# The second inverse of a block inversion taken by transposition, with 64-row and 64-column products and later modulation sums

## The chip, the cores and the metric

The kernel runs on 1 core of one Trainium2 chip. The metric is the device time of one execution in microseconds (us). Three runs of the kernel before gave 1495.1, 1495.2 and 1495.76 us, so the median is 1495.2 us.

## The reference, cut to what matters

The reference is two transformer blocks over 256 tokens of width 1024. The part that is changed belongs to the first block: an RWKV-7 recurrence of 8 heads of 64, and, beside it, the modulation vector that scales and shifts the layer norms.

```
mod = jax.nn.silu(c) @ cond_w + cond_b                   # 6 x 1024 sums over 1024
...
def step(state, inp):                                    # for each token and head
    r_t, w_t, k_t, v_t, kk_t, a_t = inp
    sa = jnp.einsum('bhvk,bhk->bhv', state, -kk_t)
    state = (state * w_t[:, :, None, :]
             + sa[..., None] * (kk_t * a_t)[:, :, None, :]
             + v_t[..., None] * k_t[:, :, None, :])
    y_t = jnp.einsum('bhvk,bhk->bhv', state, r_t)
    return state, y_t
```

Cut into two blocks of 128 tokens, the recurrence becomes matrix work. For each of 16 units (2 blocks of tokens by 8 heads) the sums `sa` solve a triangular system of 128 equations, and the kernel inverts its matrix.

## The kernel before

**The stage.** The block inversion fills roughly 105 to 216 us of the span. First `amat` (L588 to L594) makes score products for two units at a time: `AB`, from which the matrix is cut, and `AK`. A product has 128 rows, of which the 64 of the other head are zero in `AR`, and 256 columns. The DVE masks the result. The inverse is then built by doubling the size of the inverted blocks: level `li` from 0 to 6, four groups `g` of four units each. `TT` holds the inverse (transposed) and `TN` the other orientation, and both are carried along.

**One step** is one level of one group. `lvW` (L620) multiplies the level's off-diagonal part `off` by `TN` on the PE (L624), and the ACT copies the product to `W` (L625). The POOL cuts the next level's `off` (L609). `lvD` (L630) multiplies `TT` by `W` (L633) and the DVE adds it to `TN` (L634); it multiplies `W` by `TT` (L637) and the DVE adds that to `TT` (L638). At the last level, 6, `TN` is no longer needed. So there are 20 full steps (levels 1 to 5) and 4 of the last level. They are called s0 to s19 here, and a step is dated by the start of its addition to `TN`.

**Beside it.** The loop of L700 to L712 runs `lvW` one step ahead of `lvD`. After each `lvD` it takes one piece of `side()` (L668): first the `AK` score products, then transposes to token order (L649, L683), then the products `akv` (L658) of `AK` with values `vN`. After every second one it calls `modblk` (L309): a DMA of 512 KB into one of the three buffers of `wraw`, and a DVE multiplication with a running sum (L307). At `k == 10` it also does the layer norm of the convolution branch (L289 to L301 and L713 to L720), with three table loads on the ACT.

**Order.** Each engine runs its instructions strictly in an order that is fixed when the program is built. It is not the order in which the code is written: a scheduler sets it, so most of the 24 sums of L307 stand earlier than the loop calls them. A float32 product of 128 columns is two matmul records in the trace, and a transpose is one.

Of the kernel before, what the change touches and what calls it, by code (L numbers as in the profile page):

```python
# [15 lines left out]
AF = mybir.ActivationFunctionType  # L16
OP = mybir.AluOpType
AX = mybir.AxisListType

P = 128  # L20
T = 256
# [130 lines left out]
def r3(ap, b):  # L152
    return ap.rearrange("p (b t) -> p b t", b=b)
# [3 lines left out]
def body(ctx: ExitStack, tc: tile.TileContext, A: dict, out: bass.AP):  # L157
    nc = tc.nc
    pe, act, dve, pool, sp = nc.tensor, nc.scalar, nc.vector, nc.gpsimd, nc.sync
# [5 lines left out]
    def bank(name="bk"):  # L165
        return pp.tile([P, 512], F32, tag="bk", name=name)
# [9 lines left out]
    def con(name):  # L176
        w, o, n = CONST_OFF[name]
        return cst[w][:, o : o + n]
# [6 lines left out]
    ident, ones, bones = con("ident"), con("ones"), con("bones")  # L185
# [83 lines left out]
    def hs(h):  # L269
        return slice((h % 2) * 64, (h % 2) * 64 + 64)  # L270
# [38 lines left out]
    def modblk(b, c_row, junk):  # L309
        modmul(wraw(A["cond"][:, b]), b, c_row, junk)  # L310
# [16 lines left out]
    with ExitStack() as c1:  # L327
        pa = c1.enter_context(tc.tile_pool(name="pa", bufs=1))

        def tl(shape, name, tag=None, dt=F32, bufs=1):  # L330
            return (ph0 if tag in ("X3", "X4") else pa).tile(shape, dt, tag=tag or name, name=name, bufs=bufs)
# [57 lines left out]
        ps = bank()  # L389
# [4 lines left out]
        ps = bank()  # L394
# [86 lines left out]
        bT, ktT = X4[:, 0], X4[:, 1]  # L481
# [10 lines left out]
        AR = tl([P, 2, 4, 2, 2, P], "AR")  # L492
# [25 lines left out]
        for tb in range(2):  # L518
            ps = bank()
# [3 lines left out]
        for hp in range(4):  # L523
            ps = bank()
# [50 lines left out]
        for hp in range(4):  # L575
            ps = bank()
# [8 lines left out]
        AB = tl([P, 16, 2, P], "ABt", "AB")  # L585
        mskb = con("msk")[:, None, :].to_broadcast([P, 2, 256])

        def amat(src, dst, u0):  # L588
            ps = bank()
            for uu in range(2):  # L590
                u = u0 + uu
                tb, h = u // 8, u % 8
                pe.matmul(ps[:, uu * T : (uu + 1) * T], src[:, h // 2, tb * P : (tb + 1) * P], AR[:, h % 2, h // 2, tb].rearrange("p a t -> p (a t)"), start=True, stop=True)
            dve.tensor_tensor(dst[:, u0 : u0 + 2].rearrange("p u a t -> p u (a t)"), r3(ps, 2), mskb, op=OP.mult)  # L594


        TT = tl([P, 16, P], "TT", "X1")
        TN = tl([P, 16, P], "TN", "X2")
        W = tl([P, 16, P], "W", "X3")
# [3 lines left out]
        def gsl(g):  # L603
            return slice(g * 4, g * 4 + 4)

        def lv_off(li, g):
            off = tl([P, 4, P], "off", bufs=4)
            lv = con("lvl")[:, li * P : li * P + P]
            pool.tensor_tensor(off, AB[:, gsl(g), 0, :], lv[:, None, :].to_broadcast([P, 4, P]), op=OP.mult)  # L609
            offs[li, g] = off  # L610

        def lv0(g):
            off = offs[0, g]
            dve.tensor_tensor(TT[:, gsl(g)], off, idb, op=OP.add)
            ps = bank()
            for uu in range(4):
                pe.matmul(ps[:, uu * P : (uu + 1) * P], off[:, uu], ident, start=True, stop=True)
            dve.tensor_tensor(TN[:, gsl(g)], r3(ps, 4), idb, op=OP.add)

        def lvW(li, g):  # L620
# [8 lines left out]
        def lvD(li, g):  # L629
            if li < 6:  # L630
                ps2 = bank()
                for uu in range(4):
                    pe.matmul(ps2[:, uu * P : (uu + 1) * P], TT[:, g * 4 + uu], W[:, g * 4 + uu], start=True, stop=True)  # L633
                dve.tensor_tensor(TN[:, gsl(g)], TN[:, gsl(g)], r3(ps2, 4), op=OP.add)  # L634
            ps1 = bank()
            for uu in range(4):
                pe.matmul(ps1[:, uu * P : (uu + 1) * P], W[:, g * 4 + uu], TT[:, g * 4 + uu], start=True, stop=True)  # L637
            dve.tensor_tensor(TT[:, gsl(g)], TT[:, gsl(g)], r3(ps1, 4), op=OP.add)  # L638


        vN = tl([P, 2, 512], "vN")
        bN = tl([P, 512], "bN")
        kN = tl([P, 512], "kN")
        RH0 = tl([P, 8, 64], "RH0")

        def to_tok(srcs, dst):
            ps = bank()
            for hp in range(4):
                pe.transpose(ps[:, hp * P : (hp + 1) * P], srcs(hp), ident)  # L649
            act.activation(dst, ps, AF.Copy)  # L650

        def akv(g):
            ps = bank()
            tb = g // 2
            for uu in range(4):
                u = g * 4 + uu
                hp = (u % 8) // 2
                pe.matmul(ps[:, uu * P : (uu + 1) * P], AK[:, u, 0], vN[:, tb, hp * P : (hp + 1) * P], start=True, stop=True)  # L658
            h0 = (g % 2) * 4
            for pr in range(2):  # L660
                src = ps.rearrange("p (h r n) -> p h r n", h=2, r=4)[:, :, 3 * pr]
                if tb == 0:
                    dst = RH0[:, h0 : h0 + 4].rearrange("p (h r) n -> p h r n", r=2)[:, :, pr]
                else:
                    dst = RH1[:, h0 : h0 + 4].rearrange("p (h r) x n -> p h r x n", r=2)[:, :, pr, 1]
                act.activation(dst, src, AF.Copy)

        def side():  # L668

            for u0 in range(0, 16, 2):  # L670
                amat(ktT, AK, u0)
                yield
            for tb in range(2):
                to_tok(lambda hp: vT[:, hp, tb * P : (tb + 1) * P], vN[:, tb])
                yield
            to_tok(lambda hp: bT[:, hp, 0:P], bN)
            yield
            to_tok(lambda hp: ktT[:, hp, 0:P], kN)
            yield
            for pr in range(2):  # L680
                ps = bank()
                for hp in range(4):
                    pe.transpose(ps[:, hp * P : (hp + 1) * P], AR[:, pr, hp, 1, 0], ident)  # L683
                act.activation(RH1.rearrange("p (h r) x n -> p r h x n", r=2)[:, pr, :, 0], ps.rearrange("p (h r n) -> p r h n", h=4, r=2)[:, pr], AF.Copy)
                yield
            for g in range(4):
                akv(g)
                yield

        for u0 in range(0, 16, 4):  # L690
            amat(bT, AB, u0)
            amat(bT, AB, u0 + 2)
            lv_off(0, u0 // 4)
        sd = side()
        for g in range(4):
# [4 lines left out]
        AK = tl([P, 16, 2, P], "AKt", "AK")  # L700
        RH1 = tl([P, 8, 2, 64], "RH1")
# [3 lines left out]
        for k, (li, g) in enumerate(todo):  # L705
            if k + 1 < len(todo):
                lvW(*todo[k + 1])
            lvD(li, g)
            next(sd, None)
            if k % 2:  # L710
                modblk(next(mrest), c_row, junk)
            if k == 10:  # L712

                xcc, sqc = tl([P, 4, T], "xcc", "vT"), tl([P, 4, T], "sqc", "ug")
                rstdc = layer_norm(pa, yc, xcc, sqc, 4, "conv")
                ychi, yclo = tl([P, 4, T], "ychi", "yc", F32R), tl([P, 4, T], "yclo", "ug", F32R)
                for b in range(4):
                    dve.tensor_tensor(xcc[:, b], xcc[:, b], rstdc, op=OP.mult)
                    act.activation(xcc[:, b], xcc[:, b], AF.Silu, scale=col("conv_ln_g", b), bias=col("conv_ln_b", b))
                    asplit(ychi[:, b], yclo[:, b], xcc[:, b])  # L720
# [9 lines left out]
        HG = tl([P, 16, 2, 64], "HG", "X4")  # L730
        for g in range(4):
            ps = bank()
            for uu in range(4):
                u = g * 4 + uu
                h = u % 8
                if g < 2:
                    rhs = RH0[:, h - h % 2 : h - h % 2 + 2].rearrange("p a n -> p (a n)")
                else:
                    rhs = RH1[:, h].rearrange("p a n -> p (a n)")
                pe.matmul(ps[:, uu * P : (uu + 1) * P], TT[:, u], rhs, start=True, stop=True)  # L740
            if g < 2:
                for pr in range(2):
                    src = ps.rearrange("p (h r n) -> p h r n", h=2, r=4)[:, :, 3 * pr]
                    act.activation(HG[:, g * 4 : g * 4 + 4].rearrange("p (h r) x n -> p h r x n", r=2)[:, :, pr, 1], src, AF.Copy)
            else:
                act.activation(HG[:, g * 4 : g * 4 + 4].rearrange("p u a n -> p u (a n)"), r3(ps, 4), AF.Copy)


        Sb = tl([P, 4, P], "Sb", "RH0")
# [2 lines left out]
        ps = bank()  # L752
        for hp in range(4):
            o = ps[:, hp * P : (hp + 1) * P]
# [8 lines left out]
        ps = bank()  # L763
# [8 lines left out]
        for tb in range(2):  # L772
            ps = bank()
            for h in range(8):
                u = tb * 8 + h
                o = ps[hs(h), (h // 2) * P : (h // 2 + 1) * P]
# [3 lines left out]
        ps = bank()  # L780
# [63 lines left out]
        for tb in range(2):  # L844
            ps = bank()
# [16 lines left out]
    with ExitStack() as c2:  # L862
# [189 lines left out]
        for g in range(NEXP // 4):  # L1052
            tg = ("X3", "X4")[g % 2]
            zs = ph0.tile([P, 2, 4, T], F32R, tag=tg, name="zs")
            for half in range(2):
                j = 4 * g + 2 * half
                src = ZGa[:, j : j + 2] if j < NZA else ZGb[:, j - NZA : j - NZA + 2]
# [14 lines left out]
        for hb in range(4):  # L1072
            ps = bank()
# [11 lines left out]
    with ExitStack() as c3:  # L1085
# [338 lines left out]
        ps = bank()  # L1424
# [34 lines left out]
```

## Time and profile before

| what | value |
|---|---|
| median of three runs | 1495.2 us |
| profiled execution, its own time | 1492.37 us |
| its span | 1490.7 us |
| PE busy | 1426.4 us (96%) |
| DVE busy | 1059.5 us (71%) |
| ACT busy | 767.2 us (51%) |
| POOL busy | 151.4 us (10%) |
| mean granted TensorE clock | 0.99 |

The profile is of one execution. Its own time is 1.7 us above its span (1492.37 less 1490.7), and 2.8 us below the median of the runs. PE is the matrix engine and PEld its weight loads, DVE the vector engine, ACT the scalar engine, POOL GpSimd. Busy shares over the whole span say little about one stage, so the rows further down are of the stage that is changed.

### The profile page before, as it was taken

What the parts mean: (1) busy time and instruction counts of PE and PEld (TensorE: products, weight loads), DVE (VectorE), ACT (ScalarE), POOL (GpSimd) and SP (SyncE); (2) the same over time, 40 slices, a digit from 0 to 9 for tenths busy, and PEclk for the clock granted to TensorE, in tenths of its full rate; (3) what the DMA queues carried; (4) which work ended last, traced back from release to release, by engine and by line L of the source; (5) the groups of instructions that cost most, each with busy time, mean ns of one, the idle gap of its engine ahead of it and who ended that gap; (6) DMA issues with size and microseconds to landing.
All of it is one profiled execution on the core that took longest, in us unless ns stands there. A gap on an engine that the chain in (4) does not pass through costs nothing.

```text
span 1490.7 us, 26031 instructions
## 1 busy us (share of the span) xinstructions
PE 1426.4 (96%) x10381; PEld 1314.7 (88%) x10381; DVE 1059.5 (71%) x1875; ACT 767.2 (51%) x1205; POOL 151.4 (10%) x107
## 2 busy tenths in 40 slices
PE   8999899898889999999999999999998999899997
PEld 6887798798889999999988888888887989699997
DVE  7779836599975677878865566655556855598886
ACT  3731436845355555444454444544446655675654
POOL 0115310145342000000000000000002000000000
PEclk9999999999999999999999999999999999999999
DMA  9665403253456455455556667756652434256562
GB/s 384 204 203 194 143 30 99 89 169 126 142 169 197 162 166 165 160 162 167 165 177 196 199 228 227 229 192 195 196 191 97 154 124 140 77 186 191 186 196 86
DMA packets 71865, 252.09 MB, mean 169 GB/s; under 512 B 7982, under 2 KB 11967, under 8 KB 70848
## 3 DMA queue, kind: packets, MB, share of 16 engines
q1 hardware_dynamic: 68990, 245.39, 50.6%
q10 hardware_dynamic: 2754, 5.05, 1.0%
q8 instruction: 81, 1.33, 0.4%
q14 instruction: 40, 0.33, 0.1%
HBM read 248.24 MB, written 2.16 MB: 168 GB/s over the span
## 4 chain that ended last, share of the span: by engine, by line
PE 76%; DVE 14%; ACT 4%; issue 2%; DMA 2%; POOL 0%; DVEq 0%; SPq 0%; ACTq 0%; POOLq 0%
PE bk L1049 22%; PE bk L210 15%; PE bk L211 15%; PE bk L213 14%; DVE junk L307 2%; DVE wlo L199 2%; PE bk L289 1%; ACT whi L198 1%; PE bk L981 1%; DVE scr L877 1%; PE bk L301 1%; PE bk L982 1%; DMA wraw<-in_cond_dram 1%; DVE eq L939 1%; PE bk L637 1%
## 5 line engine op out<-in xcount | busy, mean ns | idle before, releaser
L198 ACT ACTIVATE whi<-wraw 128x1024 fp32r<-128x1024 f32 x400 | 423.4, 1060 | 471.7 <-PE bk L211 213.8
L199 DVE TENSOR_TENSOR wlo<-wraw,whi 128x1024 fp32r<-128x1024 f32 x374 | 471.6, 1262 | 256.1 <-ACT whi L198 253.2
L210 PE MATMUL bk<-hhi,whi 128*128 128x256 f32 x1152 | 287.9, 287 | 0.0
L211 PE MATMUL bk<-hlo,whi 128*128 128x256 f32 x1152 | 285.6, 285 | 2.1 <-DVE hlo L274 2.1
L1049 PE MATMUL bk<-whi,zs 128*128 128x512 f32 x1024 | 253.2, 390 | 1.8 <-ACT zs L273 1.7
L1049 PEld LDWEIGHTS bk<-whi,zs 128*128 128x128 f32 x1024 | 192.1, 188 | 42.3 <-ACT zs L273 1.9
L211 PEld LDWEIGHTS bk<-hlo,whi 128*128 128x128 f32 x1152 | 222.5, 193 | 2.4 <-DVE hlo L274 2.3
L210 PEld LDWEIGHTS bk<-hhi,whi 128*128 128x128 f32 x1152 | 222.2, 193 | 0.0
L213 PE MATMUL bk<-hhi,wlo 128*128 128x256 f32 x1152 | 162.8, 284 | 12.9 <-DVE wlo L199 10.2
L213 PEld LDWEIGHTS bk<-hhi,wlo 128*128 128x128 f32 x1152 | 148.8, 192 | 14.7 <-DVE wlo L199 11.6
L210 PE MATMUL bk<-hi,whi 128*128 128x256 f32 x560 | 139.8, 290 | 5.2 <-ACT hi L256 5.1
L211 PE MATMUL bk<-lo,whi 128*128 128x256 f32 x560 | 138.1, 286 | 0.0
L1049 PE MATMUL bk<-wlo,zs 128*128 128x512 f32 x512 | 136.9, 389 | 0.0
L1049 PEld LDWEIGHTS bk<-wlo,zs 128*128 128x128 f32 x512 | 96.1, 188 | 20.1 <-DVE wlo L199 0.2
L210 PEld LDWEIGHTS bk<-hi,whi 128*128 128x128 f32 x560 | 106.3, 191 | 8.0 <-ACT hi L256 6.3
L211 PEld LDWEIGHTS bk<-lo,whi 128*128 128x128 f32 x560 | 106.5, 191 | 1.2 <-DVE lo L257 0.2
L213 PE MATMUL bk<-hi,wlo 128*128 128x256 f32 x560 | 76.8, 279 | 0.0
L199 POOL TENSOR_TENSOR wlo<-wraw,whi 128x1024 fp32r<-128x1024 f32 x26 | 68.2, 2624 | 61.9 <-ACT whi L198 61.9
L213 PEld LDWEIGHTS bk<-hi,wlo 128*128 128x128 f32 x560 | 70.2, 188 | 0.0
L1122 POOL MEMSET mq<- 64x1024 f32 x2 | 1.9, 945 | 656.1 <-PE bk L1077 656.0
L307 DVE SCALAR_TENSOR_TENSOR junk<-wraw,c_row 128x1024 bf16<-128x1024 f32 x32 | 43.8, 1368 | 23.7 <-DMA wraw<-in_cond_dram 23.6
L609 POOL TENSOR_TENSOR off<-ABt,cst 128x512 f32<-128x512 f32 x28 | 39.2, 1407 | 68.8 <-PE bk L624 53.1
(524 smaller groups left out, 2207.8 us busy)
## 6 DMA issues: line engine op xcount, KB each, us to landing
wraw<-in_u_dram SPq DMA_DIRECT2D x128, 512.0 KB, 3.5
wraw<-in_v_dram SPq DMA_DIRECT2D x128, 512.0 KB, 4.3
wraw<-in_w_up_dram SPq DMA_DIRECT2D x43, 512.0 KB, 4.2
wraw<-in_w_in_dram SPq DMA_DIRECT2D x42, 512.0 KB, 4.1
wraw<-in_cond_dram SPq DMA_DIRECT2D x32, 512.0 KB, 4.3
wraw<-in_w_down_dram SPq DMA_DIRECT2D x22, 512.0 KB, 4.2
wraw<-in_w_out_dram SPq DMA_DIRECT2D x16, 512.0 KB, 3.5
wraw<-in_wq_dram SPq DMA_DIRECT2D x16, 512.0 KB, 4.1
```

The source lines that it names most:

```text
L198: act.activation(hi, raw, AF.Copy)
L199: (sub or dve).tensor_tensor(lo, raw, hi, op=OP.subtract)
L210: pe.matmul(o, w, ahi, start=first, stop=False)
L211: pe.matmul(o, w, alo, start=False, stop=False)
L213: pe.matmul(o, wl[:, k * P : (k + 1) * P], ahi, start=False, stop=last)
L289: pe.matmul(o, lhs, x3[:, b], start=b == 0, stop=b == n - 1)
L301: pe.matmul(ps2[:, :T], ones, sq[:, b], start=b == 0, stop=b == n - 1)
L307: dve.scalar_tensor_tensor(junk, w, 1.0, c_row, op0=OP.mult, op1=OP.mult, accum_out=mod[:, b : b + 1])
L609: pool.tensor_tensor(off, AB[:, gsl(g), 0, :], lv[:, None, :].to_broadcast([P, 4, P]), op=OP.mult)
L637: pe.matmul(ps1[:, uu * P : (uu + 1) * P], W[:, g * 4 + uu], TT[:, g * 4 + uu], start=True, stop=True)
L877: dve.match_replace(scr, v[:, 0:8], x, -3.0e38)
L1049: pe.matmul(y2[tb][half], z[:, tb * P : (tb + 1) * P], w[:, half * 512 : half * 512 + 512], start=first and k == 0, stop=last and k == 2)
```

## The change

Five things are done, all in this stage. After the first addition, the new `TT` of levels 1 to 5 is no longer computed by a product and a DVE addition: it is the transpose of the new `TN`, taken by the PE and copied by the ACT. Level 0 makes `TN` by a transpose in place of a product with the identity. `amat` treats four units at a time and contracts only the 64 rows of the head, even heads into one bank and odd heads into another. `akv` and the first half of the last products (`RH0`) use the 64 columns of one head in place of 128, so one copy serves where two did. In the loop, the modulation sums are called at every step from `k = 8` on, and the layer norm at `k == 8`.

```
         def amat(src, dst, u0):
-            ps = bank()
-            for uu in range(2):
+
+            pse, pso = bank(), bank()
+            for uu in range(4):
                 u = u0 + uu
                 tb, h = u // 8, u % 8
-                pe.matmul(ps[:, uu * T : (uu + 1) * T], src[:, h // 2, tb * P : (tb + 1) * P], AR[:, h % 2, h // 2, tb].rearrange("p a t -> p (a t)"), start=True, stop=True)
-            dve.tensor_tensor(dst[:, u0 : u0 + 2].rearrange("p u a t -> p u (a t)"), r3(ps, 2), mskb, op=OP.mult)
+                o = (pse, pso)[h % 2][:, (uu // 2) * T : (uu // 2 + 1) * T]
+                pe.matmul(o, src[hs(h), h // 2, tb * P : (tb + 1) * P], AR[hs(h), h % 2, h // 2, tb].rearrange("p a t -> p (a t)"), start=True, stop=True)
+            for r, ps in enumerate((pse, pso)):
+                d = dst[:, u0 : u0 + 4].rearrange("p (q r) a t -> p q r (a t)", r=2)[:, :, r]
+                dve.tensor_tensor(d, r3(ps, 2), mskb, op=OP.mult)
...
-                pe.matmul(ps[:, uu * P : (uu + 1) * P], off[:, uu], ident, start=True, stop=True)
+                pe.transpose(ps[:, uu * P : (uu + 1) * P], off[:, uu], ident)
...
-                pe.matmul(ps1[:, uu * P : (uu + 1) * P], W[:, g * 4 + uu], TT[:, g * 4 + uu], start=True, stop=True)
-            dve.tensor_tensor(TT[:, gsl(g)], TT[:, gsl(g)], r3(ps1, 4), op=OP.add)
+                o = ps1[:, uu * P : (uu + 1) * P]
+                if li < 6:
+                    pe.transpose(o, TN[:, g * 4 + uu], ident)
+                else:
+                    pe.matmul(o, W[:, g * 4 + uu], TT[:, g * 4 + uu], start=True, stop=True)
+            if li < 6:
+                act.activation(TT[:, gsl(g)], r3(ps1, 4), AF.Copy)
+            else:
+                dve.tensor_tensor(TT[:, gsl(g)], TT[:, gsl(g)], r3(ps1, 4), op=OP.add)
...
-                pe.matmul(ps[:, uu * P : (uu + 1) * P], AK[:, u, 0], vN[:, tb, hp * P : (hp + 1) * P], start=True, stop=True)
+                h = u % 8
+                pe.matmul(ps[:, uu * 64 : uu * 64 + 64], AK[:, u, 0], vN[:, tb, h * 64 : h * 64 + 64], start=True, stop=True)
...
-            for u0 in range(0, 16, 2):
+            for u0 in range(0, 16, 4):
                 amat(ktT, AK, u0)
...
-            if k % 2:
+            if k >= 8:
                 modblk(next(mrest), c_row, junk)
-            if k == 10:
+            if k == 8:
...
+            n = 64 if g < 2 else P
...
+                rhs = RH0[:, h] if g < 2 else RH1[:, h].rearrange("p a n -> p (a n)")
+                pe.matmul(ps[:, uu * n : (uu + 1) * n], TT[:, u], rhs, start=True, stop=True)
```

What this does to the order of the PE is seen at the first steps with `AK` products. These are the rows of before: `lvW` of the step ahead (L624), the two products of `lvD` (L633, L637), then two of the 16 `AK` products (L593).

```order
L624 MATMUL bk<-TN,off 128x128 x4
L633 MATMUL bk<-W,TT 128x128 x4
L637 MATMUL bk<-TT,W 128x128 x4
L593 MATMUL bk<-AR,X_374 128x256 x2
L624 MATMUL bk<-TN,off 128x128 x4
```

And these are the same rows of the PE in the changed kernel, where L628 is `lvW`, L637 the first product of `lvD`, L643 the transpose of `TN`, and L595 the `AK` products:

```order
L628 MATMUL bk<-TN,off 128x128 x4
L637 MATMUL bk<-W,TT 128x128 x4
L643 MATMUL bk<-cst_65,TN 128x128 x4
L595 MATMUL bk<-AR,X_374 128x256 x4
L628 MATMUL bk<-TN,off 128x128 x4
```

L643 stands right behind L637 in all 20 full steps, and reads the `TN` that the DVE writes from L637's bank; the work that does not need it (`AK`, the next `lvW`) stands behind it.

On the DVE, these are the rows of before from the last `TN` of level 0 (L618) over the additions of s0 and s1 (L634 to `TN`, L638 to `TT`), the mask of `AK` (L594) and the modulation sums (L307):

```order
L618 TENSOR_TENSOR TN<-bk,cst_65 128x512
L307 SCALAR_TENSOR_TENSOR junk,mod<-wraw,c_row 128x1024 x2
L634 TENSOR_TENSOR TN<-TN,bk 128x512
L638 TENSOR_TENSOR TT<-TT,bk 128x512
L594 TENSOR_TENSOR AKt<-bk,cst_127 128x512
L307 SCALAR_TENSOR_TENSOR junk,mod<-wraw,c_row 128x1024
L634 TENSOR_TENSOR TN<-TN,bk 128x512
L638 TENSOR_TENSOR TT<-TT,bk 128x512
```

And these are the rows of the changed kernel from the last `TN` of level 0 (L622) over s0 and s1 (L638 is now the addition to `TN`, L598 the mask of `AK`):

```order
L622 TENSOR_TENSOR TN<-bk,cst_65 128x512
L317 TENSOR_TENSOR mod<-mod,cols 128x8
L730 TENSOR_SCALAR mod<-mod 128x8
L307 SCALAR_TENSOR_TENSOR junk,mod<-wraw,c_row 128x1024
L638 TENSOR_TENSOR TN<-TN,bk 128x512
L307 SCALAR_TENSOR_TENSOR junk,mod<-wraw,c_row 128x1024 x2
L598 TENSOR_TENSOR AKt<-bk,cst_127 128x2x256 x2
L307 SCALAR_TENSOR_TENSOR junk,mod<-wraw,c_row 128x1024
L638 TENSOR_TENSOR TN<-TN,bk 128x512
```

The additions to `TT` are gone, and three sums of L307 stand between one addition to `TN` and the next, for each of the five gaps from s0 to s5; before, it was one or two. All 24 sums stand ahead of s5 here, though the code calls them later; before, the last one stood ahead of s9. From L756 on (`Sb` and all that follows) the orders of both kernels are the same on every engine, and SP's and POOL's orders are the same throughout.

## Rows read from the trace of the kernel before

**Rows 1.** Windows of the stage: us, each engine's busy us (instructions), granted clock, DMA share, GB/s.

```profile
137.00:154.70 17.70, 17.58 (x139) 16.87 (x138) 17.70 (x29) 2.41 (x5) 6.25 (x4) 1.00 0.64 206
173.40:176.40 3.00, 3.00 (x7) 2.41 (x8) 0.44 (x2) 2.18 (x4) 0.00 (x0) 0.52 0.24 94
183.90:187.00 3.10, 1.28 (x11) 1.09 (x10) 2.27 (x6) 2.80 (x7) 1.22 (x1) 1.00 0.00 0
187.00:191.00 4.00, 4.00 (x24) 4.00 (x23) 1.37 (x2) 0.38 (x1) 0.00 (x0) 0.57 0.00 0
191.00:207.00 16.00, 16.00 (x146) 16.00 (x145) 6.19 (x9) 4.77 (x13) 5.46 (x5) 1.00 0.01 2
```

**Rows 2.** Timeline of late steps: start, length, engine, line, operation [idle before <-releaser].

```profile
203.26 0.97 PEld L658 LDWEIGHTS bk<-vN,AKt 128*128 128x128 f32 x8
...
204.16 0.97 PEld L624 LDWEIGHTS bk<-TN,off 128*128 128x128 f32 x8
...
205.05 0.97 PEld L633 LDWEIGHTS bk<-W,TT 128*128 128x128 f32 x8
205.16 1.06 PE L633 MATMUL bk<-W,TT 128*128 128x128 f32 x8
...
206.25 0.69 DVE L634 TENSOR_TENSOR TN<-TN,bk 128x512 f32<-128x512 f32 x1 [1.99 <-PE bk L633]
...
208.93 0.69 DVE L634 TENSOR_TENSOR TN<-TN,bk 128x512 f32<-128x512 f32 x1 [1.10 <-PE bk L633]
```

**Rows 3.** Timeline: DVE additions at s0 and s8, and PE's waits for the DVE.

```profile
131.44 0.68 DVE L618 TENSOR_TENSOR TN<-bk,cst 128x512 f32<-128x512 f32 x1
132.18 0.97 PEld L637 LDWEIGHTS bk<-TT,W 128*128 128x128 f32 x8 [1.18 <-DVE TN L618]
...
135.79 0.68 DVE L634 TENSOR_TENSOR TN<-TN,bk 128x512 f32<-128x512 f32 x1
136.40 0.68 DVE L638 TENSOR_TENSOR TT<-TT,bk 128x512 f32<-128x512 f32 x1
...
164.37 0.68 DVE L634 TENSOR_TENSOR TN<-TN,bk 128x512 f32<-128x512 f32 x1
```

**Rows 4.** Timeline: a transpose and the product behind it; AB products; 64-column-weight products.

```profile
105.60 7.07 PE L593 MATMUL bk<-AR,X 128*128 128x256 f32 x32
...
160.23 0.47 PEld L649 LDWEIGHTS bk<-cst,vT 128*128 128x128 f32 x4
160.67 0.97 PEld L624 LDWEIGHTS bk<-TN,off 128*128 128x128 f32 x8
...
221.45 1.09 PE L765 MATMUL bk<-ABt,HG 128*64 128x128 f32 x16
```

**Rows 5.** Timeline: modulation sums on the DVE, with the ends of two and their successors' waits.

```profile
119.45 2.11 DVE L307 SCALAR_TENSOR_TENSOR junk<-wraw,c_row 128x1024 bf16<-128x1024 f32 x1
...
127.87 0.08 DVE L307 DVE_READ_ACCUMULATOR junk<-wraw,c_row 128x1 f32 x1
...
132.42 1.23 DVE L307 SCALAR_TENSOR_TENSOR junk<-wraw,c_row 128x1024 bf16<-128x1024 f32 x1 [0.30 <-DMA wraw<-in_cond_dram]
133.57 0.08 DVE L307 DVE_READ_ACCUMULATOR junk<-wraw,c_row 128x1 f32 x1
```

**Rows 6.** Timeline of the layer norm between the steps, and the slow steps behind it.

```profile
167.67 1.89 PE L289 MATMUL bk<-yc,cst 128*128 128x256 f32 x8
...
177.10 0.47 ACT L284 ACTIVATE rstd_conv<-bk,cst 128x256 f32<-128x256 f32 x1 [1.51 <-PE bk L301]
...
180.41 2.33 DVE L718 TENSOR_TENSOR xcc<-xcc,rstd_conv 128x256 f32<-128x256 f32 x4 [0.84 <-ACT rstd_conv L285]
...
184.90 0.57 ACT L650 ACTIVATE kN<-bk 128x512 f32<-128x512 f32 x1
...
189.39 1.64 PE L624 MATMUL bk<-TN,off 128*128 128x128 f32 x8
```

**Rows 7.** Timeline of the stage's end.

```profile
215.99 3.74 PE L740 MATMUL bk<-RH,TT 128*128 128x128 f32 x32
```

More of the change, by code (lines that the diff above doesn't have):

```diff
@@ L656, in akv @@
                 u = g * 4 + uu
-                hp = (u % 8) // 2
-                pe.matmul(ps[:, uu * P : (uu + 1) * P], AK[:, u, 0], vN[:, tb, hp * P : (hp + 1) * P], start=True, stop=True)
+                h = u % 8
+                pe.matmul(ps[:, uu * 64 : uu * 64 + 64], AK[:, u, 0], vN[:, tb, h * 64 : h * 64 + 64], start=True, stop=True)
             h0 = (g % 2) * 4
[L660 to L666, printed above, removed]
+            dst = RH0[:, h0 : h0 + 4] if tb == 0 else RH1[:, h0 : h0 + 4, 1]
+            act.activation(dst, r3(ps[:, 0:256], 4), AF.Copy)
         def side():
-            for u0 in range(0, 16, 2):
+            for u0 in range(0, 16, 4):
                 amat(ktT, AK, u0)
@@ L691, in body @@
             amat(bT, AB, u0)
-            amat(bT, AB, u0 + 2)
             lv_off(0, u0 // 4)
@@ L735, in body @@
                 h = u % 8
[L736 to L746, printed above, removed]
+                rhs = RH0[:, h] if g < 2 else RH1[:, h].rearrange("p a n -> p (a n)")
+                pe.matmul(ps[:, uu * n : (uu + 1) * n], TT[:, u], rhs, start=True, stop=True)
+            dst = HG[:, g * 4 : g * 4 + 4, 1] if g < 2 else HG[:, g * 4 : g * 4 + 4].rearrange("p u a n -> p u (a n)")
+            act.activation(dst, r3(ps[:, 0 : 4 * n], 4), AF.Copy)
         Sb = tl([P, 4, P], "Sb", "RH0")
```

## The prediction

> **What bounds the kernel now.** I first read the windows of the stage. From 137 to 154.7 us the PE is busy for 17.58 of 17.70 us and the DVE for all of it, and from 191 to 207 the PE for all of it, with the DVE at 6.19 of 16 [rows 1]. So the first half of the stage is held by PE and DVE together, and the second by the PE alone. Then I read the timeline of single steps. Late in the stage the PE starts a group of four products every 0.89 us (203.26, 204.16, 205.05) and never waits [rows 2]. A full step is three groups, 2.68 us, and 3.57 us with the four products of `akv`. The addition to `TN` starts at 206.25, only 0.03 after the product ends, and lasts 0.69; but nothing on the PE needs it for three steps, so it costs nothing now. What counts for the change is therefore not how long each engine works, but who waits for whom once the order is another.
>
> **The change, part by part.** I date the 20 full steps s0 to s19 by the start of the addition to `TN`: before, s0 at 135.79, s8 at 164.37, s19 at 208.93 [rows 2, 3].
>
> *What is removed.* On the DVE, 20 additions to `TT`, each 0.61 (135.79 to 136.40 [rows 3]): 12.2 us. On the PE, the second product of 20 steps at 0.89 becomes four transposes at 0.44 (160.23 to 160.67 [rows 4]): 20 x 0.45 = 9 us. Four groups of level 0 save the same 0.45 each, and four `akv` groups, at half the columns, 0.45 each; the first two of the last four groups save 0.9 together. The ACT gets 20 copies of about 0.6, and has room outside the layer norm.
>
> *What is added: a wait in each full step.* The transposes read the new `TN`, and stand right behind the product from which the DVE makes it. A group starts loading weights at 205.05, its product's addition starts at 206.25, 1.20 later, and lasts 0.69 [rows 2]; the PE then starts 0.06 after the DVE's end (131.44 + 0.68 = 132.12, then 132.18 [rows 3]). So the transposes start 1.20 + 0.69 + 0.06 = 1.95 after the product, instead of 0.89: a wait of 1.06. Queued behind them on the PE are the side work and the next `lvW`, and so `W`, `off` and everything else. A step is then 0.89 (`lvW`) + 1.95 + 0.44 = 3.28 us against 2.68, and 3.73 against 3.57 where 0.45 of `akv` or of transposes to token order goes along. What the removed product saves is less than the wait.
>
> *Start, until s0.* The sums of L307 run at (132.42 - 119.45) / 6 = 2.16 us each there, held by their buffers [rows 5]. Before, eight of them lie between 119.45 and s0, now six: s0 comes at 119.45 + 6 x 2.16 = 132.4, 3.4 earlier.
>
> *s0 to s5.* The order puts three sums, two masks of `AK` and one addition between s and the next. The DVE's own work is 3 x 1.15 + 3 x 0.61 = 5.3 us. Each of the three buffers is used once in a step: 4.5 us from the end of a sum to the next one on its buffer (127.95 to 132.42) and 1.15 for the sum, 5.7 us [rows 5]. Where POOL works beside it a sum takes up to 2.11, and three at the pace of 2.16 make 6.5. Between 5.3 and 6.5 I take 5.9. The PE needs less: 0.75 for the wait, 0.44, the four `AK` products, 0.89, and 1.20 for the product up to its addition. Of 64-row products before has none. The `AB` products cost 7.07 / 32 = 0.22 a record, 1.77 for four; products with 64 columns of weights cost 1.09 / 16 = 0.07 a record at most, against 0.89 / 8 = 0.11 for a full one, since two run at once [rows 2, 4]. So four take 1.77 without an overlap and 0.88 with one, and the step 5.1 or 4.2: hidden behind the DVE either way. I take the lower value, as its nearest row is the one that also uses half of the array, and keep both. Five steps: s5 at 132.4 + 5 x 5.9 = 161.9.
>
> *s5 to s8.* Three steps at 3.73: s8 at 173.1, against 164.37. The stage is 8.7 us behind there, with all the DVE's savings taken: the sums that stood between additions while the PE worked now stand while it waits.
>
> *s8 to s12, with the layer norm.* From s8: wait and transposes 1.2, L689 0.45, the sums of L289 to 3.6 (1.89 [rows 6]), mean and squares on ACT and DVE to 5.0, L301 at full clock to 7.0, `lvW` and a product: s9 at 8.9. On the ACT, from L301's end: 177.10 to 184.90 before, 7.8 us, with the table loads, `W` and the SiLUs [rows 6]. The addition of s10 stands behind L718 (0.84 + 2.33 after the table load and exponential) and comes at 12.7. The next `W` stands behind the SiLUs, a `TT` copy and one more, and is there at 16.8; s11 at 18.0, s12 at 21.8. So s12 is at 194.9.
>
> *s12 to the end.* Two steps of 3.73 and five of 3.28: s19 at 218.8, against 208.93, +9.9. Behind s19 the transposes put 0.5 more than before ahead of the last products, and those save 0.9 of their 3.74 [rows 7]. Sum: +9.5.
>
> *The clock.* From 183.9 to 187 the PE worked 1.28 of 3.1 us at a granted 1.00; from 187 to 191 the level was the lower, 1.2 GHz (mean 0.57), and it rose once the PE had worked all of that stretch [rows 1]. At that level the four products of L624 took 1.64 instead of 1.06 [rows 2, 6]. From s0 to s5 the PE now waits 2 to 2.8 us in each step of 5.9, so I expect such stretches there: a step with the PE at half clock needs 7.5 us with overlap and 9.3 without, 1.6 to 3.4 more. I take two such steps, +3.5. The Trainium skill ("TensorE: Matmul & The Clock Gate", Part 4: PE-mode transpose) says that a transpose does not count as PE work for the clock in the same way as a product. The transposes of before lie among dense products and cannot show it; by that rule the second rival below becomes likelier.
>
> Sum: +13.0 on the profiled execution's 1492.37, 1505.4; the median of the runs is 2.8 above that execution, so 1508.2.
>
> **The rivals.**
> *The clock stays low.* If the waits keep the PE at 1.2 GHz through the stage, 15 steps after s5 cost 2.2 us more each (0.89 + 0.89 + 0.44 doubled) and five before it 1.6 to 3.4: 41 to 50 us. Rows 1 show it rising after four busy microseconds, and steps with a wait of 1.06 keep the PE working two thirds of the time; so I price half: 1495.2 + 9.5 + 22 = 1527.
> *Faster: the DVE was the bound and the transposes find `TN` ready.* For it: the DVE is full from 137 to 154.7. Then 11 of the additions, all before 172 us, give 6.7 us, nine later steps 0.45 each, `akv` 1.8 and the last products 0.9: 1495.2 - 13.4 = 1482. Against it: it needs at least 1.06 us of other PE work between the product and its transposes in the order, and there is none. Below that, the PE waits in each step.
> *No change.* The wait is there, but the sums are paced by the DVE alone (5.3 a step, 3 us less by s5), the start comes 1 us earlier, the layer norm's chain is 2.5 us shorter and the clock stays up: +9.5 - 6.5 = +3, 1498, at the edge of what counts as the same.
>
> **How the numbers follow.** A measurement of this kernel can tell about 0.2%, 3 us, from no change. The forecast of a slower kernel by 5 to 20 us gets 0.62, the low clock 0.21, no change 0.11, and faster 0.06. So slower by over 0.2% is 0.83, the same 0.11, faster 0.06. The likeliest case alone spans 1500 to 1515; to leave out no more than 2 in 10 the range goes down to the edge of no change, 1499, and up to the priced low clock, 1527.
>
> **What would show it.** In the profile after, the PE should wait for L638 (the addition to `TN`) 20 times: 1.0 to 1.1 us each late in the stage, 2 us and more between s0 and s5, ahead of L643. Late steps should be 3.3 us apart, those with `akv` 3.7, those from s0 to s5 about 6, with some of them waiting for a DMA of `cond`. s8 should fall near 173 and s19 near 219 to 222; the PE's busy time falls while the span grows, and all behind the stage is moved as one. I am wrong if the transposes start within 0.3 us of the product's end, if the steps from s0 to s5 stay below 5 us, or if late steps run at half clock.

## The result, and the profile after

The changed kernel takes 1507.27 us (median of 4 runs, 1502.6 to 1509.63) against 1495.15 for the kernel before beside it: a ratio of 1.0078 (95% interval 1.0051 to 1.0104), so it is slower by 0.5 to 1.0%. A second set of four runs gave 1508.64 (ratio 1.0094, 1.007 to 1.0119). The forecast was 1508.2. The profiled execution is the shortest of the first four: 1502.6 us, 10.2 above that of before (1492.37).

First, the page of the changed kernel, busy times by engine:

```profile
span 1500.9 us, 25828 instructions
...
PE 1418.4 (95%) x10284; PEld 1301.1 (87%) x10285; DVE 1044.1 (70%) x1855; ACT 778.7 (52%) x1219; POOL 148.6 (10%) x107
```

The PE works 8.0 us less than before and the DVE 15.4 less, and the span is 10.2 us longer. So the time is in waits. Next, the addition to `TN` (now L638): what it waited for, and who waited for it (us in total, times).

```profile
  PE bk L637: 36.3, 15
...
  PEld bk L643: 29.5, 20
```

All 20 transposes (L643) made the PE wait for the DVE, 29.5 us together at the weight loads. In the timeline, the late steps of the changed kernel, which answer to [rows 2]:

```profile
214.02 0.97 PEld L637 LDWEIGHTS bk<-W,TT 128*128 128x128 f32 x8
...
215.22 0.69 DVE L638 TENSOR_TENSOR TN<-TN,bk 128x512 f32<-128x512 f32 x1 [2.54 <-PE bk L637]
215.96 0.42 PEld L643 LDWEIGHTS bk<-cst,TN 128*128 128x128 f32 x4 [0.97 <-DVE TN L638]
...
216.35 0.97 PEld L628 LDWEIGHTS bk<-TN,off 128*128 128x128 f32 x8
...
217.24 0.97 PEld L637 LDWEIGHTS bk<-W,TT 128*128 128x128 f32 x8
...
218.45 0.69 DVE L638 TENSOR_TENSOR TN<-TN,bk 128x512 f32<-128x512 f32 x1 [2.54 <-PE bk L637]
```

The addition starts 1.20 us after its product's first load, lasts 0.69, and the transposes load 0.05 later: 1.94 behind the product, where the next work used to follow after 0.89. A step is 217.24 - 214.02 = 3.22 us; it was 2.68. The DVE stands idle too, 2.54 of each 3.2 us, so both engines wait in turn.

The steps from s0 to s5 on the DVE, which answer to [rows 3] and [rows 5]:

```profile
131.45 0.69 DVE L638 TENSOR_TENSOR TN<-TN,bk 128x512 f32<-128x512 f32 x1
...
134.23 1.23 DVE L307 SCALAR_TENSOR_TENSOR junk<-wraw,c_row 128x1024 bf16<-128x1024 f32 x1 [0.88 <-DMA wraw<-in_cond_dram]
...
138.29 0.69 DVE L638 TENSOR_TENSOR TN<-TN,bk 128x512 f32<-128x512 f32 x1 [0.49 <-PE bk L637]
...
161.65 0.68 DVE L638 TENSOR_TENSOR TN<-TN,bk 128x512 f32<-128x512 f32 x1
...
172.63 0.69 DVE L638 TENSOR_TENSOR TN<-TN,bk 128x512 f32<-128x512 f32 x1 [2.97 <-PE bk L637]
...
194.09 0.69 DVE L638 TENSOR_TENSOR TN<-TN,bk 128x512 f32<-128x512 f32 x1 [3.43 <-PE bk L637]
198.21 0.69 DVE L638 TENSOR_TENSOR TN<-TN,bk 128x512 f32<-128x512 f32 x1 [3.43 <-PE bk L637]
```

s0 comes at 131.45, s5 at 161.65: five steps of 6.04 us, each with three sums, some of which wait for their DMA. s8 is at 172.63 (before 164.37) and s19 at 218.45 (before 208.93). The last two rows are s12 and s13, a step with `akv`: 4.12 us.

The windows of the changed kernel (columns as in [rows 1]):

```profile
131.00:162.00 31.00, 21.63 (x136) 17.29 (x136) 27.49 (x47) 6.46 (x11) 7.02 (x5) 0.84 0.80 260
...
203.00:219.00 16.00, 12.21 (x100) 11.27 (x100) 3.33 (x6) 5.97 (x10) 4.36 (x4) 1.00 0.00 1
...
130.00:138.00 8.00, 5.81 (x28) 4.66 (x28) 6.88 (x14) 1.19 (x2) 0.53 (x1) 0.57 0.82 275
```

From s0 to s5 the PE is busy 21.6 of 31 us, at a mean clock of 0.84; late in the stage 12.2 of 16, at full clock.

Products, layer norm and the stage's end, again by the timeline of the PE and its weight loads, beside [rows 4], [rows 6] and [rows 7]:

```profile
105.74 3.72 PE L595 MATMUL bk<-AR,X 64*128 64x256 f32 x32
...
139.62 1.14 PE L595 MATMUL bk<-AR,X 64*128 64x256 f32 x8
140.69 1.16 PE L628 MATMUL bk<-TN,off 128*128 128x128 f32 x8
...
177.58 2.00 PE L301 MATMUL bk<-sqc,cst 128*128 128x256 f32 x8 [1.38 <-ACT sqc L300]
...
186.18 0.97 PEld L669 LDWEIGHTS bk<-vN,AKt 128*128 128x128 f32 x8
186.29 1.00 PE L669 MATMUL bk<-vN,AKt 128*128 128x64 f32 x8
187.07 0.97 PEld L628 LDWEIGHTS bk<-TN,off 128*128 128x128 f32 x8
187.13 1.11 PE L628 MATMUL bk<-TN,off 128*128 128x128 f32 x8
...
226.06 3.74 PE L743 MATMUL bk<-RH,TT 128*128 128x64 f32 x32
```

The 64-row products take half the time (3.72 us for 32 records against 7.07). The 64-column products save nothing: the product behind `akv` starts 187.13 - 186.29 = 0.84 us after it, but the weight loads of the two start 187.07 - 186.18 = 0.89 apart, as at 128 columns, and the last products take 3.74 as before. They start 10.1 us later than before (226.06 against 215.99), and that is what is left at the end.

### The profile page after: what moved, and what is told of

Read it like the earlier page. It is cut to its first block, busy times and chain, and to the rows that moved or that the text cites. A ratio compares the mean times of both kernels' runs of the same rounds, so it can differ in the third digit from the quotient of the medians.

```text
span 1500.9 us, 25828 instructions
## 1 busy us (share of the span) xinstructions
PE 1418.4 (95%) x10284; PEld 1301.1 (87%) x10285; DVE 1044.1 (70%) x1855; ACT 778.7 (52%) x1219; POOL 148.6 (10%) x107
## 4 chain that ended last, share of the span: by engine, by line
PE 79%; DVE 11%; ACT 4%; DMA 2%; issue 2%; POOL 1%; DVEq 0%; SPq 0%; ACTq 0%; POOLq 0%
PE bk L1048 23%; PE bk L210 15%; PE bk L211 14%; PE bk L213 14%; DVE junk L307 2%; DVE wlo L199 2%; PE bk L289 1%; PE bk L628 1%; ACT whi L198 1%; PE bk L980 1%; PE bk L981 1%; DMA wraw<-in_cond_dram 1%; PE bk L301 1%; PE bk L637 1%; POOL wlo L199 1%
## 5 line engine op out<-in xcount | busy, mean ns | idle before, releaser
L198 ACT ACTIVATE whi<-wraw 128x1024 fp32r<-128x1024 f32 x400 | 423.6, 1060 | 470.6 <-PE bk L211 214.4
L199 DVE TENSOR_TENSOR wlo<-wraw,whi 128x1024 fp32r<-128x1024 f32 x374 | 471.0, 1260 | 256.8 <-ACT whi L198 252.7
L199 POOL TENSOR_TENSOR wlo<-wraw,whi 128x1024 fp32r<-128x1024 f32 x26 | 67.4, 2592 | 61.3 <-ACT whi L198 55.4
L307 DVE SCALAR_TENSOR_TENSOR junk<-wraw,c_row 128x1024 bf16<-128x1024 f32 x32 | 43.0, 1344 | 25.7 <-DMA wraw<-in_cond_dram 25.5
```

The source lines that it names most:

```text
L198: act.activation(hi, raw, AF.Copy)
L199: (sub or dve).tensor_tensor(lo, raw, hi, op=OP.subtract)
L307: dve.scalar_tensor_tensor(junk, w, 1.0, c_row, op0=OP.mult, op1=OP.mult, accum_out=mod[:, b : b + 1])
```

## The experiments

The theory is the wait: the PE stands behind transposes that read what the DVE has just begun to make. Rival 1 is the place of the modulation sums, rival 2 the 64-row and 64-column products, rival 3 the clock. Each median stands with its ratio to the kernel before on the same chip.

### The transposes one step later

```
-            ps1 = bank()
...
+        def lvT(li, g):
+            ps1 = bank()
...
             lvD(li, g)
+            if k:
+                lvT(*todo[k - 1])
             next(sd, None)
...
+        lvT(*todo[-1])
```

> The changed kernel with each step's transposes and TT copy put one step later on the PE, behind the next step's first product. If the wait for the DVE is the cause (theory), the PE no longer waits for the addition to TN, late steps fall from 3.23 us to about 0.89 + 0.89 + 0.44 = 2.2 us, and the time falls by 15 to 20 us from the changed kernel, to 1487 to 1493, below the kernel before. If the three sums between additions at s0 to s5 are the cause (rival 1) or the 64-row and 64-column products (rival 2), the transposes' place changes less than 4 us: 1503 or more.

Measured: 1492.79 us, ratio 0.9986 (0.9971 to 1.0001), some 14 us less than the changed kernel. The interval reaches 1, so that it is faster than the kernel before, as expected, is not shown. The windows show late steps without a wait, and the list of waits a PE that stands behind `TN` 7 times for 7.5 us, not 20 times for 29.5:

```profile
194.00:206.00 12.00, 12.00 (x110) 12.00 (x109) 4.13 (x6) 6.21 (x11) 4.83 (x5) 1.00 0.00 1
...
PEld bk L645 <- DVE TN L638: 7.5, 7, 2.3
```

The additions to `TN` stand at 196.37, 198.60 and 200.82: 2.22 us a step, against 3.22. No sum stands there in either kernel, so this difference is the wait alone. Rival 2 falls as cause of the loss, since all its products are still in this kernel. Rival 1 is not separated by this run, because the new place of the transposes changed the order of the sums too. From s0 on the DVE has two of them between additions where the changed kernel has three:

```profile
131.22 0.68 DVE L638 TENSOR_TENSOR TN<-TN,bk 128x512 f32<-128x512 f32 x1
131.82 1.50 DVE L307 SCALAR_TENSOR_TENSOR junk<-wraw,c_row 128x1024 bf16<-128x1024 f32 x1
...
133.25 1.28 DVE L598 TENSOR_TENSOR AKt<-bk,cst 128x512 f32<-128x512 f32 x2
134.46 1.21 DVE L307 SCALAR_TENSOR_TENSOR junk<-wraw,c_row 128x1024 bf16<-128x1024 f32 x1
...
135.60 0.68 DVE L638 TENSOR_TENSOR TN<-TN,bk 128x512 f32<-128x512 f32 x1
...
151.99 0.68 DVE L638 TENSOR_TENSOR TN<-TN,bk 128x512 f32<-128x512 f32 x1
```

s0 to s5 take 20.77 us here against 30.20, and that is 9.4 of the 13.2 us by which s19 comes earlier (205.27 against 218.45). How these 9.4 divide between the wait and the third sum stays open: three sums stand in most of these gaps in every kernel here that has the transposes in place, and in no gap of the others.

The time reached only the upper end of what was expected. Its timeline shows a longer wait in the layer norm:

```profile
165.31 1.06 ACT L198 ACTIVATE whi<-wraw 128x1024 fp32r<-128x1024 f32 x1 [4.49 <-DMA wraw<-in_w_out_dram]
166.27 0.37 ACT L296 ACTIVATE mean_conv<-bk 128x256 f32<-128x256 f32 x1
166.40 1.23 DVE L199 TENSOR_TENSOR wlo<-wraw,whi 128x1024 fp32r<-128x1024 f32 x1 [2.34 <-ACT whi L198]
167.54 1.43 DVE L299 TENSOR_TENSOR xcc<-yc,mean_conv 128x256 f32<-128x256 f32 x4
...
168.46 3.78 PE L301 MATMUL bk<-sqc,cst 128*128 128x256 f32 x8 [6.45 <-ACT sqc L300]
```

The order puts the split of `w_out`, which waits for its DMA, ahead of the norm's mean on the ACT (L198 before L296) and ahead of its subtraction on the DVE (L199 before L299). The faster steps now arrive there before the DMA does, and the PE idles 6.45 us ahead of L301. The kernel before has a wait there too, of 3.83 us:

```profile
173.39 3.68 PE L301 MATMUL bk<-sqc,cst 128*128 128x256 f32 x8 [3.83 <-ACT sqc L300]
```

### The transposes alone

The kernel before, with only `TT` of levels 1 to 5 by transposition, in place:

```
+                if li < 6:
+                    pe.transpose(o, TN[:, g * 4 + uu], ident)
...
+            if li < 6:
+                act.activation(TT[:, gsl(g)], r3(ps1, 4), AF.Copy)
```

> The kernel before with one edit: the new TT of levels 1 to 5 by transposition and an ACT copy. Theory (the wait): it is about as slow as the changed kernel or a little slower, 1503 to 1512, with the PE waiting 20 times behind the first product. Rival 2 (the 64-row and 64-column products are the cause): near 1495 or faster. Rival 1 (the sums' place in the code): near 1495, since the calls stand as before.

Measured: 1516.08 us, ratio 1.0148 (1.0127 to 1.017): 22 us slower than before, more than the whole change and 4 us above what was expected. The PE waits for `TN` in every step (up to 225 us 19 times, 32.1 us in all). First a row of the list of waits, then additions to `TN` from the timeline:

```profile
PEld bk L639 <- DVE TN L634: 32.1, 19, 8.7
...
135.47 0.68 DVE L634 TENSOR_TENSOR TN<-TN,bk 128x512 f32<-128x512 f32 x1
...
165.06 0.68 DVE L634 TENSOR_TENSOR TN<-TN,bk 128x512 f32<-128x512 f32 x1
...
169.13 0.69 DVE L634 TENSOR_TENSOR TN<-TN,bk 128x512 f32<-128x512 f32 x1 [1.09 <-PE bk L633]
```

Against the changed kernel s0 is 4.0 us later (135.47), as two more sums stand ahead of it, and behind s5 (165.06) three steps still carry `AK` products, at 4.1 us each. The stage ends 17.1 us later than before (`Sb` on the DVE at 238.76 against 221.63); in this profile 7.8 us more were lost behind the stage, for a reason that stays open. This one edit carries more than all of the loss; the others give some of it back.

### All but the transposes

The changed kernel with the second product and its DVE addition back in all levels:

```
-                if li < 6:
-                    pe.transpose(o, TN[:, g * 4 + uu], ident)
...
+            dve.tensor_tensor(TT[:, gsl(g)], TT[:, gsl(g)], r3(ps1, 4), op=OP.add)
```

> The changed kernel with the second product and the DVE addition to TT put back; everything else of the change stays. Theory: no wait, so faster than before by what level 0, the 64-row products and the last products save, 2 to 6 us: 1489 to 1493. Rival 2: still 1503 or more. Rival 1: still 1500 or more, as the sums are called late.

Measured: 1495.29 us, ratio 1.0015 (1.0003 to 1.0026). The loss is gone, as the theory says, and rival 2, and rival 1 in the form that late calls cost the time, miss by 5 us and more. The expected saving of 2 to 6 us is absent too. The timeline shows a long wait in the layer norm again:

```profile
167.91 1.42 DVE L299 TENSOR_TENSOR xcc<-yc,mean_conv 128x256 f32<-128x256 f32 x4
...
169.04 1.06 ACT L198 ACTIVATE whi<-wraw 128x1024 fp32r<-128x1024 f32 x1 [5.13 <-DMA wraw<-in_w_out_dram]
...
170.46 3.78 PE L301 MATMUL bk<-sqc,cst 128*128 128x256 f32 x8 [6.96 <-ACT sqc L300]
```

Here the subtraction (L299) stands behind sums on the DVE, and the squares (L300, at 170.01) behind the split of `w_out` on the ACT (L198), which waits for its DMA.

### The sums and the layer norm called as before

```
-            if k >= 8:
+            if k % 2:
                 modblk(next(mrest), c_row, junk)
-            if k == 8:
+            if k == 10:
```

> The changed kernel with the modulation sums called at every second step and the layer norm at k == 10, as before. The order of the sums on the DVE then is the one of the changed kernel, only the layer norm moves two steps back. Theory: the time of the changed kernel within 3 us, 1503 to 1510. Rival 1 in the form that the late calls cost the time: 1500 or less.

Measured: 1509.93 us, ratio 1.0107 (1.008 to 1.0135): no different from the changed kernel. The PE stands idle 1.38 us ahead of L301 with either place of the layer norm, and the sums stand on the DVE where they stood. So late calls are not the cause; the order of the sums itself was not varied by this run.

### Late transposes, with the layer norm as before

Both edits together: the late transposes, and the calls of the run above.

> The late transposes of the run before, with the modulation sums and the layer norm called as in the kernel before. There L301 stood idle for 6.5 us, since the order on the DVE put the split of w_out, which waits for its DMA, ahead of the layer norm's subtraction; here two steps stand between. If that is what ate the gain, the idle time before L301 falls to 2 us or less and the time to 1484 to 1490. If the gain is lost elsewhere (the transposes' own cost, the 64-column products), it stays at 1491 to 1495.

Measured: 1482.94 us (1478.03 to 1486.27), ratio 0.9919 (0.9894 to 0.9944): faster than both kernels, by 12 and 24 us, a little more than expected. The layer norm's wait on the PE is short:

```profile
170.43 1.99 PE L301 MATMUL bk<-sqc,cst 128*128 128x256 f32 x8 [1.38 <-ACT sqc L300]
```

With the sums left at `k >= 8` and only the norm at `k == 10`, the program has the same order on all five engines as this one. So against the first experiment it is the norm's place alone that gives 10 us, and calling the sums later does nothing.

### The wait filled with other products

```
                 dve.tensor_tensor(TN[:, gsl(g)], TN[:, gsl(g)], r3(ps2, 4), op=OP.add)
+                pw = bank("fill")
+                for uu in range(4):
+                    pe.matmul(pw[:, (uu % 4) * P : (uu % 4 + 1) * P], ident, ident, start=True, stop=True)
```

> The changed kernel with four more products of the identity with itself, 0.89 us of PE work, between each step's first product and its transposes; their result is not used. Theory: the PE has 1.06 us of wait there, so late steps stay at 3.2 to 3.3 us though they hold 40% more PE work, and the time stays within 3 us of the changed kernel, 1503 to 1510, or falls by up to 4 where the fuller PE keeps the 2.4 GHz level. If the PE were the bound by its work (no wait), 20 times 0.89 would add 18 us: 1525.

> As the run before with eight more products, 1.78 us, in each gap. Theory: 1.06 of it is covered by the wait, the rest shows: late steps near 4.05 us, and the fifteen steps after s5 cost 0.8 each, +12 against four products; between s0 and s5, where the wait is 2 us and more, nothing: 1514 to 1521. If the PE were the bound by its work: 36 us, 1543.

Measured: 1503.1 us with four products (ratio 1.0067, 1.0047 to 1.0086) and 1517.45 with eight (1.0172, 1.0144 to 1.0199). First the timeline with four, then that with eight:

```profile
215.72 0.97 PEld L641 LDWEIGHTS fill<-cst 128*128 128x128 f32 x8
...
216.03 0.69 DVE L638 TENSOR_TENSOR TN<-TN,bk 128x512 f32<-128x512 f32 x1 [2.53 <-PE bk L637]
218.95 0.97 PEld L641 LDWEIGHTS fill<-cst 128*128 128x128 f32 x8
```

```profile
219.03 1.06 PE L637 MATMUL bk<-W,TT 128*128 128x128 f32 x8
219.93 1.95 PE L641 MATMUL fill<-cst 128*128 128x128 f32 x16
...
223.04 1.06 PE L637 MATMUL bk<-W,TT 128*128 128x128 f32 x8
```

Four products fit into the wait: the step stays at 218.95 - 215.72 = 3.23 us. Eight do not: 223.04 - 219.03 = 4.01, 0.79 more, and the 14 us between the two runs are close to the 12 that were expected. The wait of about 1 us is thus measured from both sides. The runs with four products lay only 2.1 us apart (1502.45 to 1504.57). Their median is 4 to 6 us below those of the changed kernel, but in the profile the stage ends no earlier (`Sb` at 232.42 against 231.62).

The run with four products also speaks to rival 3. The windows of the changed kernel had a mean clock of 0.84 from 131 to 162 us; here it is 0.93:

```profile
131.00:162.00 31.00, 24.14 (x179) 20.53 (x180) 26.97 (x46) 6.46 (x11) 6.49 (x5) 0.93 0.79 260
```

Yet s0 to s5 take 30.07 us (130.88 to 160.95) against 30.20. So the lower clock is not what makes these steps long.

### The transposes alone, one step later

The kernel before with the transposition, and `lvT` as in the first experiment.

> The kernel before with the transposition alone, and each step's transposes one step later on the PE. Theory: the wait is gone, a late step falls from 2.68 to 2.23 and the DVE loses 12 us of additions, so it is faster than before by 4 to 10 us: 1485 to 1490, while the same edit with the transposes in place cost 22 us. If a transpose by itself is the loss, it stays above 1500.

Measured: 1489.31 us, ratio 0.9976 (0.9961 to 0.999). The same edit that cost 22 us in place gains some 4 when the next step's work stands between. The transposition is no loss by itself; its place is.

### The rest, with the layer norm as before

The third experiment (second product back) with `k % 2` and `k == 10`:

> All of the change but the transposition of TN (the second product and its DVE addition stay), with the sums and the layer norm called as in the kernel before. The run without that last edit was no faster than before, and stood 7 us idle ahead of L301. If the layer norm's earlier place ate the saving of level 0, the 64-row products and the last products, this is 2 to 6 us faster than before, ratio 0.996 to 0.9985. If those edits save nothing, the ratio is 0.9985 to 1.0015.

Measured: 1489.99 us, ratio 0.9967 (0.9951 to 0.9983): 5 us faster than before. With the norm's earlier place the same kernel was no faster; by the ratios the difference is 7 us. The wait ahead of L301 fell from 6.96 to 2.85 us (3.83 in the kernel before):

```profile
172.56 3.64 PE L301 MATMUL bk<-sqc,cst 128*128 128x256 f32 x8 [2.85 <-ACT sqc L300]
```

### The changed kernel again

> The changed kernel once more, beside the run above, for the spread of its time: its four first runs lay 7 us apart. If the granted clock in the waits makes the spread, its runs are again over 4 us apart and go with the mean granted clock of the run, and the kernel with 0.89 us of products in each gap (2.1 us apart) stays the steadier one. Median 1503 to 1510.

Measured: 1508.64 us (1506.72 to 1510.47), 3.8 us apart, less than expected; 13 runs of the kernel before lay up to 8 us apart in the same comparison. Nor did the times go with the clock: 1506.82 us had a mean of 0.983 and 1510.45 us one of 0.986. So the spread says nothing about the waits.

The profile of this run is of an execution 4.1 us longer than the first one (1506.72 against 1502.6). Of these, 1.4 us show at the stage's end (`Sb` at 233.04 against 231.62): the steps s4 to s6, part of them at the lower clock level, take 11.72 us against 9.37, and others less. The other 2.7 us lie behind the stage. Over all twelve profiles the part from `Sb` to the end takes between 1269.1 and 1276.8 us, with the same order of instructions on the DVE. Why it differs stays open, and a few microseconds between single executions need not come from the stage that was changed.

The stage's end by itself tells the same story as the medians. `Sb` starts at 221.63 before, 231.62 in the changed kernel, 217.75 with late transposes, 211.20 with late transposes and the norm as before, 238.76 with the transposes alone, and 221.65 with all but the transposes.

## Why the prediction was right

**The wait in each step.** Right, in place and size: 1.94 us behind the product, forecast 1.95; late steps 3.22, forecast 3.28. Between s0 and s5 the PE waited 2.1 to 2.8 us at s2, s3 and s5, as forecast, and 0.8 at s1 and s4. Moving the transposes shows that their place makes the loss, and late in the stage, where the gaps hold no sums, moving them and filling the wait show that the wait does.

**Start, and s0 to s5.** Right: s0 at 131.45 (132.4 forecast), steps of 6.04 (5.9), s5 at 161.65 (161.9). The sums, paced by DVE and buffers, stood in the wait as forecast; how much of these steps is the wait and how much the sums was not separated.

**The 64-row products.** The lower value was the better one: `AB` took 3.72 / 32 = 0.12 us a record, and the four `AK` products of a step 140.69 - 139.62 = 1.07 us at full clock, where the forecast had 0.88 or 1.77.

**The 64-column products.** Mis-sized. The step "four `akv` groups, at half the columns, 0.45 each; the first two of the last four groups save 0.9 together" came to nothing. An `akv` step took 198.21 - 194.09 = 4.12 us, not 3.73: 0.90 more than a late step without `akv`, as much as 128 columns cost before (3.57 - 2.68 = 0.89). In the window of the last products each record follows the load of its own 128 columns of weights (32 records in 3.74 us at either width).

**The layer norm.** s8 to s12 took 194.09 - 172.63 = 21.46 us, forecast 21.8. That its place, k = 8, costs nothing was true only because of the waits; in the kernels without them it costs 7 and 10 us by the ratios, which I had not seen.

**The clock.** Forecast: two steps at 1.2 GHz, +3.5. The profile shows it at that level from 130.5 to 137.3 and from 151 to 154.3; the steps there took 6.84 and 6.05 against 5.8, about 1.3 us together. The term was too large for this execution, whose +10.2 lies close to the sum without the clock (+9.5). The other three first runs are 3 to 7 us longer at granted clocks of 0.985 to 0.982 against 0.987; the one longer execution with a profile has 1.4 of its 4.1 us in the stage. That the forecast of 1508.2 came within 1 us of the median is in part luck: its +13.0 was 2.8 too much for the profiled execution, and the median lies 4.7 above that execution, not 2.8. Of the page's rule on transposes ("TensorE: Matmul & The Clock Gate", Part 4, in the Trainium skill) no harm shows late in the stage: from 203 to 219 us each step holds transposes and a wait, and the clock is 1.00 throughout. The rival that the rule makes likelier is the first of the list, the clock that stays low, not the second, as the forecast has it; late steps at full clock speak against it.

## What to carry to other kernels

Before an operation is made cheaper by deriving it from another's result, look at what stands between the two on the engine that runs both: here the saving of 0.45 us a step became a loss of 0.54, and one step of delay in the code turned it into a gain. When a stage gets faster, look again at what it waits for at its edges, since a transfer that was hidden may then come last. And where a scheduler sets the order, a call that is moved in the code may change nothing (the sums) or much (the layer norm); read the order.

## What the runs showed of the hardware

- A round trip from a PE product to a DVE addition and back to the PE took 1.94 us from the product's first weight load, of which 1.05 is not covered by the product's own loads.
- Products over 64 rows, even heads and odd heads in different halves and banks, took about half the time: 3.72 us for 32 records of 256 columns, 7.07 for those over 128 rows.
- Products of 64 columns with new weights each time took the time of 128 columns: 0.89 us from weight load to weight load for eight records at either width, and 3.74 against 3.74 for the last 32, of which half were narrowed. With late transposes an `akv` step took 3.12 us at 64 columns (191.03 to 194.15) and at 128 (189.02 to 192.14, in the transposes alone, one step later).
- A float32 transpose of 128 by 128 took 0.11 us of the PE (four in 0.39 to 0.44), half of a product.
